# Down-projection in 19 uneven runs of pairs, its first operands and weights split before the up-projection's last sums

## The chip, the cores and the metric

The kernel runs on one core of a Trainium2 chip. The metric is the device time of one execution in microseconds (us); lower is better. One program holds a whole decoder layer; the change concerns its last stage and the seam in front of it.

## The reference

The layer has three parallel branches, a gated merge and an output projection, and ends with a normalised squared-ReLU MLP. Only this end matters here (1,024 tokens, model width 1,024, hidden width 4,096):

```python
x = x + merged @ w_out[l]
h2 = rms_norm(x, norm_mlp_g[l])
x = x + jnp.square(jax.nn.relu(h2 @ w_up[l])) @ w_down[l]
```

## The kernel before

All matrix products keep fp32 accuracy by splitting each operand into a high part (a cast on ScalarE) and a low part (a subtraction on VectorE) and issuing three matmuls per product (`mm3`, L130). `split` (L110) leaves both halves to the scheduler; `split2` (L105) pins the subtraction on VectorE (`self.V`, L69) behind whatever was traced before it on that engine. Matmuls are pinned the same way (L94). Every other instruction (ScalarE's, GpSimd's, the DMA issues of SyncE's queue, SP, and VectorE's where `nc.vector` is called) is placed on its engine by a scheduler at compile time; once placed, each engine runs its list in order.

Both MLP products use Strassen-Winograd: a 2x2 block product in seven products instead of eight. A **step** is one K-pair (256 rows of the contraction) for one group of outputs: 7 products x 3 = 21 matmuls of 128x128 by 128x512.

- **Up-projection** (`wino`, L1309): 16 groups u of 4 steps. After each group, `combine` (L1328) copies the first of seven PSUM banks to SBUF on ScalarE and folds the other six with seven VectorE adds into four 128x512 blocks (tiles u and c). `use_up` (L1537) multiplies them by the row norm (on GpSimd for the last group, u = 15), applies ReLU and square on ScalarE, stores three of them (tile rq), forms four Winograd sums (`wino_t`, tile xts, L1258) and stores those too. Group u's result, seven blocks in the scratch tensor r_d, is K-pair u of the down-projection.
- **Down-projection** (`down`, L1586): 4 output groups g x 16 pairs = 64 steps. A pair's operand is loaded (`xdma`), then split (`xsplit`, tiles xd) into one of four SBUF places, chosen by pair number mod 4; a weight tile is loaded (`raw`, tile wraw), gets four Winograd sums on GpSimd (`wino_s`, L1277) and is split (`wsp`, tiles wo); there are three places for each kind. The steps are cut into **passes**: one output group over consecutive pairs, collected in seven PSUM banks. Pass p takes group p mod 4 and pairs p to p + 3, so there are 16 passes of 4, and pairs 16, 17 and 18 are pairs 0, 1 and 2 loaded a second time. At the end of a pass, seven accumulators in SBUF take up the banks: in a group's first pass three by ScalarE copies and four by VectorE adds onto the residual, which four DMAs (acc<-x1_d, traced as acc<-x_d, L1698) put there and one subtraction prepares. Eight banks are cycled, so product j + 1 of a pass needs the bank that product j of the pass before has left. In each group's last pass the sums are folded and stored; group 3's accumulators are folded ahead, at the end of pass 11, so that the very last pass has a short end.
- **Places**: SBUF space of the down stage is laid over that of the up stage. The operand place of pair 0 is in three parts, dx00, dx01 and dx02; dx02 lies on the last two up-projection weight buffers. Pairs 1, 2 and 3 lie on up operands 0, 1 and 2, which are last read in the last four up steps. Accumulators of groups 0 and 1 lie on up operand 3, those of groups 2 and 3 mostly on the tiles u, c, xts and rq.

What sets the order at the seam is therefore the scheduler: the last group's `combine`, its post-processing, the stores of r_d and the first loads and splits of the down stage are all placed by it, except that `split2` subtractions and accumulations are pinned behind what was traced before them.

Of the kernel before, what the change touches and what calls it, by code (L numbers as in the profile page):

```python
# [10 lines left out]
F32 = mybir.dt.float32  # L11
F32R = mybir.dt.float32r
AF = mybir.ActivationFunctionType
# [4 lines left out]
P = 128  # L18
# [13 lines left out]
def f32(ap):  # L32
    return ap.bitcast(F32)
# [40 lines left out]
class Layer:  # L74
# [9 lines left out]

    pinned = False
    nmm, kmm = 0, 2
    marks = {}

    def pin(self, ins):
# [6 lines left out]
    def transpose(self, out, x):  # L96
        self.pin(self.nc.tensor.transpose(out, x, self.ident))  # L97

    def other_tile(self):
        return self.pmm.tile([P, 512], F32, tag=f"mm{1 - self.nmm}", name=self.name("pr"))  # L100

# [2 lines left out]

    def split2(self, hi, lo, src):  # L105

        self.A.copy(hi, src)  # L107
        self.V.tensor_sub(lo, src, f32(hi))

    def split(self, hi, lo, src, scale=None):  # L110

        nc = self.nc
        if scale is None:
            a = nc.scalar.copy(hi, src)  # L114
            return a, nc.vector.tensor_sub(lo, src, f32(hi))  # L115
# [1142 lines left out]
    def wino_t(self, b, V):  # L1258

        G = self.nc.gpsimd  # L1260
        t = self.xtp.tile([P, 4, 512], F32, tag="xt", name=self.name("xts"))
        V.tensor_sub(t[:, 0], b[:, 0], b[:, 1])
        G.tensor_sub(t[:, 2], b[:, 2], b[:, 0])
        V.tensor_sub(t[:, 1], b[:, 2], t[:, 0])
        V.tensor_sub(t[:, 3], b[:, 3], t[:, 1])
        return t

    def wino_x(self, kp, load):
# [40 lines left out]
    def wino(self, ws, load, use, first, parts):  # L1309


        V, A = self.V, self.A
# [3 lines left out]
        raw, wsp, W = self.wino_steps([ws[u][:, kp] for u, kps in runs for kp in kps], self.wrp, self.wop, 3)  # L1316
# [11 lines left out]
        def combine(ms, psum):  # L1328

            m1, m2, m6, m7, m4, m5, m3 = ms  # L1330
            u2, c11, u3, c21 = m1, m2, m7, m4
            if psum:
                u2, c11, u3, c21 = (tl(n) for n in ("u2", "c11", "u3", "c21"))
                A.copy(u2, m1)
            V.tensor_add(c11, u2, m2)
# [5 lines left out]
            V.tensor_add(u2, u2, m3)  # L1341
            return u2, c11, u3, c21


# [1 line left out]
        n = -1  # L1346
        for r, (u, kps) in enumerate(runs):
            bank = lambda j: f"p{(7 * r + j + 4) % 8}"
            ps = [self.pw.tile([P, 512], F32, tag=bank(j), name=self.name(f"p{j}")) for j in range(7)]
# [18 lines left out]
            elif r == 2:  # L1368
# [66 lines left out]
    def tail(self):  # L1435
        tc, nc, a = self.tc, self.nc, self.a
        V, G = nc.vector, nc.gpsimd
        half = lambda d, f, hf: d[f, :, hf * 512 : (hf + 1) * 512]
# [8 lines left out]
        with ExitStack() as c0:  # L1447
# [9 lines left out]
            with ExitStack() as c1:  # L1457
                E = lambda *x, **k: c1.enter_context(tc.tile_pool(*x, **k))
                self.pmm, self.kmm, self.nmm = Banks(E, "pmm2"), 8, 3
                if True:  # L1460
# [11 lines left out]
                    hi = [[mtp.tile([P, 512], F32R, name=f"mh{k}_{hf}") for hf in range(2)] for k in range(NK)]  # L1472
                    mg, lo = {}, {}
# [43 lines left out]
            with ExitStack() as c1:  # L1517
                E = lambda *x, **k: c1.enter_context(tc.tile_pool(*x, **k))
                one_ = lambda n: E(name=n, bufs=1)
# [17 lines left out]
                def use_up(u, cs):  # L1537

                    b = self.xrp.tile([P, 4, 512], F32, tag="xr", name=self.name("rq"))
                    V_, M = (nc.vector, G) if u == 15 else (self.V, self.V)  # L1540
                    for i in (1, 3, 2, 0):
                        hf = i % 2
                        M.tensor_mul(cs[i], cs[i], rb[:, hf * 512 : (hf + 1) * 512])
                        self.A.activation(cs[i], cs[i], AF.Relu)
                        self.A.activation(b[:, i], cs[i], AF.Square)
# [3 lines left out]
                    nc.sync.dma_start(self.rd[u, :, 3:7], t)  # L1549
                    yield  # L1550

                def rstd():
# [33 lines left out]
    def down(self):  # L1586

        tc, nc, a = self.tc, self.nc, self.a
        V = nc.vector
        half = lambda d, f, hf: d[f, :, hf * 512 : (hf + 1) * 512]  # L1590
        with ExitStack() as c1:
            one_ = lambda n: c1.enter_context(tc.tile_pool(name=n, bufs=1))
# [27 lines left out]
            kp = lambda q: q if q < 16 else q - 16  # L1620
# [6 lines left out]
            raw, wsp, W = self.wino_steps([a["wdown"][g][:, kp(q)] for g, q in steps], wr, wo, 2)  # L1627
# [5 lines left out]
            def xdma(q):  # L1633

                X[q] = []
                for pool, i, n in xp[q % 4]:
                    t = pool.tile([P, n, 2, 512], F32R, tag=f"x{i}", name=self.name("xd"))
                    nc.sync.dma_start(f32(t[:, :, 1]), self.rd[kp(q), :, i : i + n])
                    X[q].append(t)

            def xsplit(q, parts=(0, 1, 2), split=self.split2):
                for i, t in enumerate(X[q]):
                    if i in parts:
                        split(t[:, :, 0], t[:, :, 1], f32(t[:, :, 1]))

            def operand(q, j):
                for t in X[q]:
                    if j < t.shape[1]:
                        return t[:, j, 0], t[:, j, 1]
                    j -= t.shape[1]  # L1650

            def side(n):
# [24 lines left out]
            n = -1  # L1677
            seen = set()
            for p, (g, qs) in enumerate(passes):
                A = acc[g]  # L1680
                new = g not in seen
                seen.add(g)
                ps = [
                    self.pw.tile([P, 512], F32, tag=f"p{(7 * (self.nwino + p) + j + 4) % 8}", name=self.name(f"p{j}"))
                    for j in range(7)
                ]
# [6 lines left out]
                    if q != qs[-1]:  # L1693
                        side(n)
                if new:

                    for j, f, hf in ((1, 0, 1), (6, 0, 0), (4, 1, 1), (5, 1, 0)):
                        nc.sync.dma_start(A[j], half(self.x1d, 2 * g + f, hf))  # L1698
                    V.tensor_sub(A[6], A[6], A[5])

                if p <= last - 4:
                    for j in range(7):
                        if new and j in (0, 2, 3):
                            A_.copy(A[j], ps[j])
                        else:
                            V.tensor_add(A[j], A[j], ps[j])
                    side(n)
                    if p == last - 4:
                        add = V.tensor_add
                        a1, a2, a6, a7, a4, a5, a3 = A  # L1710
                        add(a2, a2, a1)
                        add(a6, a6, a1)
                        add(a7, a7, a6)
                        add(a4, a4, a7)
                        add(a7, a7, a5)
                        add(a6, a6, a5)
                        add(a6, a6, a3)
                    continue
                o = lambda f, hf, t: nc.sync.dma_start(half(self.out, 2 * g + f, hf), t)
                add = V.tensor_add  # L1720
                a1, a2, a6, a7, a4, a5, a3 = A
# [15 lines left out]
                else:  # L1737

                    m1, m2, m6, m7, m4, m5, m3 = ps
# [203 lines left out]
```

## Time and profile before

| | us |
|---|---|
| median of 3 runs (2176.92 to 2179.55) | 2178.19 |
| the profiled execution, its own time | 2178.26 |
| its span, first to last instruction | 2176.5 |
| up-projection's matmuls, first start to down's first | 1541.1 to 1852.3 |
| down-projection's matmuls, first start to last end | 1852.3 to 2171.9 |

A row of a timeline is: start, length, engine, source line, operation, written tile <- read tiles, shape, count; brackets hold the idle time before the row and the instruction that ended it. Rows of `L94 ... p<-xd,wo` are down-projection matmuls; `xd` rows are operand splits, `wo` rows weight splits, `acc` rows accumulations. VectorE is DVE, ScalarE ACT, GpSimd POOL, TensorE PE; SPq is SyncE's DMA queue. A view of windows gives each engine's busy time in a stretch and PEclk, the TensorE clock granted, as a share of full speed.

### The profile page before, as it was taken

Reading aid. Unit: us, or ns where it says so; the run is one execution under the profiler, and the core shown is the slowest. Engines: PE = TensorE matmul, PEld = TensorE weight load, DVE = VectorE, ACT = ScalarE, POOL = GpSimd, SP = SyncE. Lnnn points to the kernel's source line nnn. Section 1 sums busy time; section 2 is a strip of 40 time slices with the busy share of each in tenths; the row PEclk is TensorE's granted clock in tenths of the full one; section 3 lists DMA queues with packets and bytes.
Section 4 is the critical chain, followed back from the end, with each engine's and each line's share of the span. In section 5 each row is a group of like instructions: output and inputs, shape, how many; then the busy total and the mean of one; then the engine's idle time right before and its main releaser. Section 6 shows DMA issues by size and latency. Waiting matters only on the chain.

```text
span 2176.5 us, 30687 instructions
## 1 busy us (share of the span) xinstructions
PE 2140.9 (98%) x11049; PEld 1850.3 (85%) x11049; DVE 1415.2 (65%) x2674; ACT 998.6 (46%) x1998; POOL 567.2 (26%) x736
## 2 busy tenths in 40 slices
PE   7999999999999999999999999999999999899999
PEld 5888888898899999999878888888888788688887
DVE  6644475574557787777655342645688987767789
ACT  6543354453346666666544220314444444543332
POOL 2100000000111111111031002103655674655552
PEclk9999999999999999999999999999999999999999
DMA  6115122131433333323344543426434544844444
GB/s 240 44 65 169 36 92 69 40 102 37 170 92 93 93 98 98 95 77 85 107 159 150 199 165 106 146 94 218 134 141 169 184 160 174 304 155 160 152 137 166
DMA packets 137357, 281.45 MB, mean 129 GB/s; under 512 B 13137, under 2 KB 29814, under 8 KB 135158
## 3 DMA queue, kind: packets, MB, share of 16 engines
q1 hardware_dynamic: 130870, 259.58, 37.4%
q10 hardware_dynamic: 6336, 19.93, 2.3%
q8 instruction: 87, 1.43, 0.3%
q14 instruction: 64, 0.52, 0.1%
HBM read 182.95 MB, written 71.34 MB: 117 GB/s over the span
## 4 chain that ended last, share of the span: by engine, by line
PE 88%; DVE 4%; DMA 2%; ACT 2%; issue 1%; POOL 1%; SPq 0%; DVEq 0%; ACTq 0%; POOLq 0%
PE mm L94 52%; PE p L94 23%; PE sc L94 6%; PE po L94 3%; PE tp L97 3%; DVE acc L69 1%; PE pr L97 1%; DVE u L69 1%; DVE wo L69 1%; DMA hx<-hc_d 0%; DVE c L69 0%; PE tp L94 0%; DVE w L115 0%; DMA ngb<-g_dng 0%; DMA xd<-r_d 0%
## 5 line engine op out<-in xcount | busy, mean ns | idle before, releaser
L94 PE MATMUL mm<-w,hT 128*128 128x384 f32 (+3 forms) x2496 | 468.7, 330 | 0.7 <-DVE dsg L118 0.7
L94 PE MATMUL mm<-hT,w 128*128 128x512 f32 x1680 | 408.1, 393 | 1.2 <-ACT gt L492 1.2
L94 PEld LDWEIGHTS mm<-w,hT 128*128 128x128 f32 x2496 | 388.6, 189 | 10.9 <-DVE dsg L118 0.9
L94 PEld LDWEIGHTS mm<-hT,w 128*128 128x128 f32 x1680 | 308.3, 188 | 61.4 <-ACT gt L492 1.7
L94 PE MATMUL p<-xd,wo 128*128 128x512 f32 x1344 | 311.4, 393 | 8.2 <-DVE acc L69 1.9
L94 PEld LDWEIGHTS p<-xd,wo 128*128 128x128 f32 x1344 | 254.1, 190 | 65.3 <-DVE xd L69 2.6
L94 PE MATMUL p<-xo,wo 128*128 128x512 f32 x1344 | 307.0, 390 | 1.5 <-DVE u L69 1.5
L94 PEld LDWEIGHTS p<-xo,wo 128*128 128x128 f32 x1344 | 251.6, 188 | 55.6 <-DVE u L69 3.1
L94 PE MATMUL mm<-kt,w 128*128 128x512 f32 x1152 | 261.5, 389 | 0.0
L94 PEld LDWEIGHTS mm<-kt,w 128*128 128x128 f32 x1152 | 216.1, 188 | 45.2 <-DVE kt L115 0.3
L107 ACT CAST wo<-wraw 128x896 fp32r<-128x896 f32 x124 | 116.9, 945 | 217.6 <-PE p L94 105.2
L114 ACT CAST w<-raw 128x256 fp32r<-128x256 f32 (+3 forms) x272 | 139.8, 546 | 140.4 <-PE mm L94 112.0
L115 DVE TENSOR_TENSOR w<-raw,w 128x256 fp32r<-128x256 f32 (+3 forms) x272 | 158.7, 607 | 51.7 <-ACT w L114 51.0
L69 DVE TENSOR_TENSOR wo<-wraw,wo 128x896 fp32r<-128x896 f32 x124 | 144.8, 1182 | 56.6 <-ACT wo L107 56.6
L1280 POOL TENSOR_TENSOR wraw<-wraw 128x128 f32<-128x128 f32 x128 | 94.4, 738 | 240.0 <-DMA wraw<-in_wdown 101.2
L1029 ACT ACTIVATE dpe<-sc,dst,drr 128x256 f32<-128x256 f32 (+7 forms) x128 | 106.7, 834 | 96.7 <-DVE dst L1025 93.6
L140 POOL TENSOR_SCALAR hss<-hss 128x4 f32<-128x4 f32 x8 | 4.1, 515 | 409.0 <-ACT mscr L774 409.0
L1021 DVE CUSTOM_DVE_ANT_0 sc<-sc,tmask 128x256 f32<-128x256 f32 (+7 forms) x128 | 97.1, 759 | 13.8 <-PE sc L94 13.1
L1283 POOL TENSOR_TENSOR wraw<-wraw 128x128 f32<-128x128 f32 x128 | 90.0, 703 | 10.0
L94 PE MATMUL sc<-dk,dq 128*128 128x512 f32 (+3 forms) x384 | 91.9, 347 | 0.0
L107 ACT CAST xd<-xd 128x1536 fp32r<-128x1536 f32 (+2 forms) x38 | 58.3, 1535 | 65.8 <-DMA xd<-r_d 65.8
L1282 POOL TENSOR_TENSOR wraw<-wraw 128x128 f32<-128x128 f32 x128 | 87.1, 681 | 0.0
(313 smaller groups left out, 3078.8 us busy)
## 6 DMA issues: line engine op xcount, KB each, us to landing
dk<-dsg SPq DMA_DIRECT2D x64, 256.0 KB, 4.2
wraw<-in_wup SPq DMA_DIRECT2D x64, 256.0 KB, 3.0
r_d<-xts SPq DMA_DIRECT2D x16, 1024.0 KB, 4.1
wraw<-in_wdown SPq DMA_DIRECT2D x64, 256.0 KB, 3.0
xd<-r_d SPq DMA_DIRECT2D x19, 768.0 KB, 7.1
xd<-r_d SPq DMA_DIRECT2D x14, 1024.0 KB, 6.2
raw<-in_wd SPq DMA_DIRECT2D x32, 384.0 KB, 3.3
kraw<-y SPq DMA_DIRECT2D x24, 512.0 KB, 5.3
```

The lines of the kernel that those rows point to most:

```text
L69: return self.tc.keep_in_program_order(f(*a, **k))
L94: self.pin(self.nc.tensor.matmul(out, l, r, start=start, stop=stop))
L97: self.pin(self.nc.tensor.transpose(out, x, self.ident))
L107: self.A.copy(hi, src)
L114: a = nc.scalar.copy(hi, src)
L115: return a, nc.vector.tensor_sub(lo, src, f32(hi))
L140: g.tensor_scalar(r, ss, 1.0 / width, EPS, op0=ALU.mult, op1=ALU.add)
L1021: V.tensor_tensor_reduce(out=sc[:, 0:n], in0=sc[:, 0:n], in1=self.tmask[:, D - n : D], scale=1.0, scalar=-3.0e38, op0=ALU.add, op1=ALU.max ...
L1029: nc.scalar.activation(pe[c][:, 0:n], sc[:, 0:n], AF.Exp, bias=t8[:, 2 + c : 3 + c], scale=rr[:, i, c : c + 1], accum_out=t8[:, 4 + c : 5 ...
L1280: G.tensor_add(r[:, 4], r[:, 0], r[:, 3])
L1282: G.tensor_sub(r[:, 6], r[:, 1], r[:, 0])
L1283: G.tensor_sub(r[:, 7], r[:, 2], r[:, 5])
```

## The change

- The passes become 19, of 2, 2, 3, 4, then 3, 4, 4, 4, then 4, 4, 4, 4, then 3, 3, 2, and last 4, 3, 3, 4 pairs. Every pair is loaded once; the second loads of pairs 0, 1 and 2 go.
- Explicit steps for the operand splits (`SPLIT`) and for group 3's early folding (`FOLD`) take the place of fixed distances.
- dx02 moves to free space at the end; a dummy tile (dfree) fills its old place. Pair 0's three parts are split behind the Winograd sums of up groups 10, 11 and 12.
- Order edges (`behind`: at compile time, an engine's list gets the first argument after the second): pair 1's load before the store of up group 14; pair 1's casts before `combine`'s first copy, and weight 1's subtraction before its first add, for the last up group; weight 2's subtraction after its last add; the last group's four ReLUs after the first pass's ScalarE copies and its Winograd sums after that pass's VectorE adds; the residual loads of groups 0 and 1 before the store of up group 15, and pair 3's load after that store. The residual of group g + 1 is loaded one pass ahead.

```diff
+    def behind(self, ins, first):
+        self.tc.add_manual_dep(
+            ins, first.name,
+            mybir.DependencyInfo(mybir.DependencyClass.NoSync, mybir.DependencyReason.DATA), reason="order",
+        )
...
-            x02, wr = one_("dx02"), Ring(wr)
+            one_("dfree").tile([P, 2048], F32, name="dfree")
+            wr = Ring(wr)
             wo = Ring([one_(f"dwo{i}") for i in range(3)])
-            x00 = one_("dx00")
+            x00, x02 = one_("dx00"), one_("dx02")
...
-            passes = [(p % 4, tuple(range(p, 4 + p))) for p in range(16)]
+            to = lambda g, lo, hi: (g, tuple(range(lo, hi + 1)))
+            passes = [to(0, 0, 1), to(1, 0, 1), to(2, 0, 2), to(3, 0, 3)]
+            passes += [to(0, 2, 4), to(1, 2, 5), to(2, 3, 6), to(3, 4, 7)]
+            passes += [to(0, 5, 8), to(1, 6, 9), to(2, 7, 10), to(3, 8, 11)]
+            passes += [to(0, 9, 11), to(1, 10, 12), to(2, 11, 12)]
+            passes += [to(0, 12, 15), to(1, 13, 15), to(2, 13, 15), to(3, 12, 15)]
...
-                    if q >= 3 and n == use1[q] - 3:
-                        xsplit(q, (0,))
-                    if q >= 3 and n == use1[q] - 2:
-                        xsplit(q, (1, 2))
+                    for i, at in enumerate(SPLIT.get(q, ())):
+                        if n == at:
+                            xsplit(q, (0,) if i == 0 else (1, 2))
+                for t, s in FOLD.get(n, ()):
+                    V.tensor_add(acc[3][t], acc[3][t], acc[3][s])
...
+            SPLIT = {2: (3, 4), 3: (7, 8), 4: (10, 11), 5: (13, 14)}
+            SPLIT.update({q: (4 * q - 7, 4 * q - 6) for q in range(6, 13)})
+            SPLIT.update({13: (45, 46), 14: (48, 49), 15: (50, 51)})
             xdma(0)
             raw()
             raw()
-            xsplit(0, split=self.split)
+            turned = self.turned[-16:]
+            for i, u in enumerate((10, 11, 12)):
+                xsplit(0, (i,), self.split, turned[u][1])
             wsp(0, self.split, False)
-            xdma(1)
+            self.behind(self.stored[14], xdma(1))
             xsplit(1, split=self.split)
+            self.behind(self.first_copy, self.cast)
             wsp(0)
+            self.behind(self.first_add, self.sub)
+            wsp(0)
+            self.behind(self.sub, self.last_add)
             xdma(2)
-            xsplit(2, (0,))
-            wsp(0)
-            xsplit(2, (1, 2))
-            xdma(3)
...
                 if new:
-                    for j, f, hf in ((1, 0, 1), (6, 0, 0), (4, 1, 1), (5, 1, 0)):
-                        nc.sync.dma_start(A[j], half(self.x1d, 2 * g + f, hf))
+                    if g == 0:
+                        residual(0)
+                        loaded = residual(1)
+                        self.behind(self.stored[15], loaded)
+                        with tc.issue_after(self.stored[15]):
+                            xdma(3)
+                    elif g < 3:
+                        residual(g + 1)
                     V.tensor_sub(A[6], A[6], A[5])
...
+                    if p == 0:
+                        for i in range(4):
+                            self.behind(self.relus[15, i], c.ins)
+                        self.behind(self.turned[-1][0], v.ins)
                     side(n)
```

More of the change, by code (lines that the diff above doesn't have):

```diff
@@ L86 @@
     nmm, kmm = 0, 2
+    turned, stored, relus = [], {}, {}
     marks = {}
@@ L105, in split2 @@
     def split2(self, hi, lo, src):
-        self.A.copy(hi, src)
-        self.V.tensor_sub(lo, src, f32(hi))
+        self.cast = self.A.copy(hi, src).ins
+        self.sub = self.V.tensor_sub(lo, src, f32(hi)).ins
     def split(self, hi, lo, src, scale=None):
@@ L114, in split @@
             a = nc.scalar.copy(hi, src)
+            self.cast = a.ins
             return a, nc.vector.tensor_sub(lo, src, f32(hi))
@@ L1261, in wino_t @@
         t = self.xtp.tile([P, 4, 512], F32, tag="xt", name=self.name("xts"))
-        V.tensor_sub(t[:, 0], b[:, 0], b[:, 1])
+        first = V.tensor_sub(t[:, 0], b[:, 0], b[:, 1]).ins
         G.tensor_sub(t[:, 2], b[:, 2], b[:, 0])
         V.tensor_sub(t[:, 1], b[:, 2], t[:, 0])
-        V.tensor_sub(t[:, 3], b[:, 3], t[:, 1])
+        self.turned.append((first, V.tensor_sub(t[:, 3], b[:, 3], t[:, 1]).ins))
         return t
@@ L1333, in combine @@
                 u2, c11, u3, c21 = (tl(n) for n in ("u2", "c11", "u3", "c21"))
-                A.copy(u2, m1)
-            V.tensor_add(c11, u2, m2)
+                self.first_copy = A.copy(u2, m1).ins
+            self.first_add = V.tensor_add(c11, u2, m2).ins
             V.tensor_add(u2, u2, m6)
@@ L1340, in combine @@
             V.tensor_add(u2, u2, m5)
-            V.tensor_add(u2, u2, m3)
+            self.last_add = V.tensor_add(u2, u2, m3).ins
             return u2, c11, u3, c21
@@ L1618, in down @@
             acc = [accs[7 * g : 7 * g + 7] for g in range(4)]
-            kp = lambda q: q if q < 16 else q - 16
             self.pinned = True
             V, A_ = self.V, self.A
-            passes = [(p % 4, tuple(range(p, 4 + p))) for p in range(16)]
+            to = lambda g, lo, hi: (g, tuple(range(lo, hi + 1)))
[4 more added lines that the diff above has]
+            passes += [to(0, 12, 15), to(1, 13, 15), to(2, 13, 15), to(3, 12, 15)]
             last = len(passes) - 1
             steps = [(g, q) for g, qs in passes for q in qs]
-            raw, wsp, W = self.wino_steps([a["wdown"][g][:, kp(q)] for g, q in steps], wr, wo, 2)
+            raw, wsp, W = self.wino_steps([a["wdown"][g][:, q] for g, q in steps], wr, wo, 2)
             X, use1, use9 = {}, {}, {}
@@ L1637, in xdma, with xsplit @@
                     t = pool.tile([P, n, 2, 512], F32R, tag=f"x{i}", name=self.name("xd"))
-                    nc.sync.dma_start(f32(t[:, :, 1]), self.rd[kp(q), :, i : i + n])
+                    ins = nc.sync.dma_start(f32(t[:, :, 1]), self.rd[q, :, i : i + n]).ins
                     X[q].append(t)
-            def xsplit(q, parts=(0, 1, 2), split=self.split2):
+                return ins
+            def xsplit(q, parts=(0, 1, 2), split=self.split2, after=None):
                 for i, t in enumerate(X[q]):
                     if i in parts:
-                        split(t[:, :, 0], t[:, :, 1], f32(t[:, :, 1]))
+                        with tc.issue_after(after) if after else ExitStack():
+                            split(t[:, :, 0], t[:, :, 1], f32(t[:, :, 1]))
             def operand(q, j):
@@ L1650, in operand @@
                     j -= t.shape[1]
+            FOLD = {42: ((1, 0), (2, 0)), 46: ((3, 2), (4, 3)), 52: ((3, 5), (2, 5), (2, 6))}
             def side(n):
@@ L1666, in down, with residual @@
             raw()
-            xsplit(0, split=self.split)
+            turned = self.turned[-16:]
+            for i, u in enumerate((10, 11, 12)):
+                xsplit(0, (i,), self.split, turned[u][1])
             wsp(0, self.split, False)
-            xdma(1)
+            self.behind(self.stored[14], xdma(1))
             xsplit(1, split=self.split)
+            self.behind(self.first_copy, self.cast)
             wsp(0)
+            self.behind(self.first_add, self.sub)
+            wsp(0)
+            self.behind(self.sub, self.last_add)
             xdma(2)
-            xsplit(2, (0,))
-            wsp(0)
-            xsplit(2, (1, 2))
-            xdma(3)
+            def residual(g):
+                for j, f, hf in ((1, 0, 1), (6, 0, 0), (4, 1, 1), (5, 1, 0)):
+                    ins = nc.sync.dma_start(acc[g][j], half(self.x1d, 2 * g + f, hf)).ins
+                return ins
             n = -1
@@ L1703, in down @@
                         if new and j in (0, 2, 3):
-                            A_.copy(A[j], ps[j])
+                            c = A_.copy(A[j], ps[j])
                         else:
-                            V.tensor_add(A[j], A[j], ps[j])
-                    side(n)
[L1708 to L1717, printed above, removed]
+                            v = V.tensor_add(A[j], A[j], ps[j])
+                    if p == 0:
+                        for i in range(4):
+                            self.behind(self.relus[15, i], c.ins)
+                        self.behind(self.turned[-1][0], v.ins)
+                    side(n)
                     continue
```

4 lines of the change are left out of this document (2 added, 2 removed).

## The prediction, made before the changed kernel ran

> **What bounds the kernel now.** I read the page first: its share of busy time by engine says that TensorE is the engine to look at.
>
> ```profile
> span 2176.5 us, 30687 instructions
> PE 2140.9 (98%) x11049; PEld 1850.3 (85%) x11049; DVE 1415.2 (65%) x2674; ACT 998.6 (46%) x1998; POOL 567.2 (26%) x736
> ```
>
> With 98% busy nothing but a gap in the matmuls can be won, unless matmuls are removed, and the change removes none: 64 steps of 21 before and after. The second view is TensorE's timeline over the down stage.
>
> ```profile
> 1852.31 1.52 PE L94 MATMUL p<-xd,wo 128*128 128x512 f32 x6
> 1854.39 0.97 PE L94 MATMUL p<-xd,wo 128*128 128x512 f32 x3 [0.56 <-DVE c L69]
> 1856.11 2.51 PE L94 MATMUL p<-xd,wo 128*128 128x512 f32 x9 [0.76 <-POOL wraw L1281]
> 1859.04 10.52 PE L94 MATMUL p<-xd,wo 128*128 128x512 f32 x45 [0.42 <-DVE u L69]
> 1871.16 0.50 PE L94 MATMUL p<-xd,wo 128*128 128x512 f32 x1 [1.60 <-ACT wo L107]
> 1873.29 0.79 PE L94 MATMUL p<-xd,wo 128*128 128x512 f32 x1 [1.64 <-DVE xd L69]
> 1875.42 8.16 PE L94 MATMUL p<-xd,wo 128*128 128x512 f32 x25 [1.33 <-DVE wo L69]
> 1885.46 286.42 PE L94 MATMUL p<-xd,wo 128*128 128x512 f32 x1254 [1.88 <-DVE acc L69]
> ```
>
> The last row is one unbroken run of 1254 matmuls, 286.42 / 1254 = 0.2284 us each, so a step of 21 costs 4.80 us and nothing is to be won behind 1885.46 except at the very end. The 90 matmuls ahead of it should take 90 x 0.2284 = 20.56 us and take 1885.46 - 1852.31 = 33.15. **12.6 us are lost in the first four steps and the first change of pass.** By row: the first 18 matmuls take 6.73 us instead of 4.11 (2.6 lost); the next 45 take 12.12 with the gap behind them instead of 10.28 (1.8); the last 27 take 14.30 instead of 6.17 (8.1). The idle times in brackets sum only to 8.2; the rest is slow running, and the window view says why.
>
> ```profile
> 1874.00:1878.00 4.00, 2.67 (x7) 1.62 (x6) 4.00 (x4) 2.29 (x3) 1.60 (x2) 0.50 0.82 261
> ```
>
> The 0.50 is the granted clock: after three gaps in a row TensorE gets half its speed for some us. A gap costs more than its length.
>
> Third, who is late. VectorE's list at the seam:
>
> ```profile
> 1851.44 2.29 DVE L115 TENSOR_TENSOR xd<-xd 128x2048 fp32r<-128x2048 f32 x1 [0.16 <-ACT xd L114]
> 1853.65 0.68 DVE L69 TENSOR_TENSOR c<-u,p 128x512 f32<-128x512 f32 x1
> 1854.25 1.16 DVE L69 TENSOR_TENSOR wo<-wraw,wo 128x896 fp32r<-128x896 f32 x1
> 1855.33 1.47 DVE L69 TENSOR_TENSOR u<-u,p 128x512 f32<-128x512 f32 x2
> 1868.94 0.69 DVE L1262 TENSOR_TENSOR xts<-rq 128x512 f32<-128x512 f32 x1 [2.93 <-ACT rq L1545]
> 1871.23 2.01 DVE L69 TENSOR_TENSOR xd<-xd 128x1536 fp32r<-128x1536 f32 x1
> 1874.03 1.34 DVE L69 TENSOR_TENSOR wo<-wraw,wo 128x896 fp32r<-128x896 f32 x1
> 1875.29 2.54 DVE L69 TENSOR_TENSOR xd<-xd 128x2048 fp32r<-128x2048 f32 x1
> 1884.11 0.69 DVE L69 TENSOR_TENSOR acc<-acc,acc 128x512 f32<-128x512 f32 x1 [5.29 <-DMA acc<-x_d]
> ```
>
> Three stories stand here. First, the up-projection's last `combine` starts only at 1853.65, behind pair 1's split, and weight 1's split cuts in after its first add, so the banks come free late. Second, weight 3 and pair 3 are split at 1871 to 1877.8, behind the last group's post-processing, though step 3 should start at 1852.31 + 3 x 4.80 = 1866.7. Third, the end of pass 0 waits for the residual. GpSimd and SP say why the second and third are so late:
>
> ```profile
> 1832.28 0.46 POOL L1283 TENSOR_TENSOR wraw<-wraw 128x128 f32<-128x128 f32 x1
> 1863.93 2.39 POOL L1283 TENSOR_TENSOR wraw<-wraw 128x128 f32<-128x128 f32 x1
> 1866.29 1.29 POOL L1543 TENSOR_TENSOR u<-u,rb 128x512 f32<-128x512 f32 x1
> ```
>
> ```profile
> 1838.22 2.57 SPq L1638 DMA_DIRECT2D xd<-r_d  x3
> 1860.03 1.46 SPq L1638 DMA_DIRECT2D xd<-r_d  x3
> 1874.18 0.33 SPq L1549 DMA_DIRECT2D r_d<-xts  x1
> 1874.91 1.65 SPq L1294 DMA_DIRECT2D wraw<-in_wdown  x2
> 1876.61 2.05 SPq L1698 DMA_DIRECT2D acc<-x_d  x4
> ```
>
> The last multiplication of group 15 sits on GpSimd until 1866.29 behind weight sums; ScalarE's last ReLU waits for it, and the splits of weight 3 and pair 3 stand behind that ReLU in ScalarE's list. The store of group 15 blocks SP from the end of the row at 1860.03, 1861.5, to 1874.18; two weight loads and the residual's loads stand behind it.
>
> **The change part by part.**
>
> *Combine and splits at the seam.* Pair 1's casts and weight 1's subtraction now stand ahead of `combine`, then seven adds run unbroken, then weight 2's subtraction. Pair 0's third part no longer has its load among the three issued at 1838.22 nor its cast among the three here, which all end before the late split of 1851.44:
>
> ```profile
> 1847.06 4.36 ACT xd L114 x3
> ```
>
> Of the three casts the smallest goes (1024 of 4608 columns, 1.0 us), so pair 1's subtractions end near 1852.7 instead of 1853.73; weight 1's 1.16 us follow; the first add starts at 1853.9 at the worst, and some 2 us sooner if a load a fifth smaller also lands sooner. The down stage's third product (from 1852.31 + 6 x 0.2284 = 1853.7) needs that add done. Each further add takes about 0.7 us, a product 0.685, so they keep pace. Loss left: 0 to 1.0 of 2.6; I take 0.4, nearer the low end, since the load shrinks.
>
> *Short first passes.* Pairs 2 and 3 are first needed in steps 6 and 10 (at 1881 and 1900) instead of 2 and 3. Pair 3's split of 1871 to 1877.8 would be in time even unmoved. What is late next is weight 3, needed at 1866.7: its place is free after step 0 (1857.1), its cast no longer stands behind a ReLU, its subtraction stands behind the first pass's adds. The pass ends at 1861.9, the last add 0.7 later, the subtraction 1.2 later, 1863.8: 2.9 us in hand.
>
> *Residual.* Its loads need up operand 3, free at 1852.31, and are now put before the store of group 15. These are the times from issue to landing in the seam, beside 12 weight loads:
>
> ```profile
> acc<-x_d SPq DMA_DIRECT2D x16, 256.0 KB, 5.6
> wraw<-in_wdown SPq DMA_DIRECT2D x12, 256.0 KB, 5.6
> ```
>
> Four issues of 0.5 us and 5.6 to land give 1860; the first add onto them can start when product 1 of step 1 is done, 1858.5, and must not start later than 1862.5 (its bank is needed a whole step less one product on). So this stall goes, unless a weight load that waits for weight 2's subtraction is put ahead: then 1858.5 + 2 + 5.6 = 1866, 3.5 us late. I take 0.6.
>
> *New waits.* Group 15's ReLUs now follow the first pass's third ScalarE copy, its Winograd sums that pass's last add (1862.6). Both come before the multiplication that ends at 1866.29 + 1.29 = 1867.6 in the trace, so if that keeps its time, the sums start at 1868.94 and the store is issued at 1874.18 as now; if it comes sooner, some 3 us sooner. So 1871 to 1875. Queued behind it on SP: pair 3's load (needed at 1900, covered), the residual of group 2, and perhaps weight loads from 7 on. Group 2's residual needs the store landed, then its own landing; at 5.6 each that is 1882 to 1886, wanted at 1882.5 and not later than 1886.5. Weight 7, if put behind the store: 1875 + 5.6, four sums of 0.46 to 2.39 each, 2.3 for cast and subtraction: 1885 to 1892, wanted at 1885.9. Loss 0 to 6; I take 1.0, since a weight load is released by the split three weights ahead, and those of 3 and 4 come by 1866.
>
> *More passes, fewer loads.* The groups of the down stage give the prices:
>
> ```profile
> L69 DVE TENSOR_TENSOR xd<-xd 128x1536 fp32r<-128x1536 f32 (+2 forms) x38 | 74.0, 1954 | 0.7 <-ACT xd L107 0.6
> L69 DVE TENSOR_TENSOR wo<-wraw,wo 128x896 fp32r<-128x896 f32 x63 | 70.9, 1140 | 55.3 <-ACT wo L107 55.3
> L69 DVE TENSOR_TENSOR acc<-acc,p 128x512 f32<-128x512 f32 x100 | 67.1, 686 | 13.2 <-PE p L94 12.5
> ```
>
> Three more passes add 21 adds of 0.686 = 14.4 us to VectorE; the 38 parts are 17 whole pairs, 74.0 / 17 = 4.35 each, so three pairs fewer save 13.1. Net 1.3 us on an engine that has slack, but not evenly. The densest stretch is steps 42 to 49: 21 adds (14.4), 8 weights (9.1), pairs 13 and 14 (8.7), four folding adds (2.8), 35.0 of 38.4 us. Before, a pass of the last third already ran like this, with no gap in TensorE:
>
> ```profile
> 2110.00:2129.20 19.20, 19.20 (x86) 15.91 (x85) 19.00 (x22) 6.50 (x6) 9.46 (x16) 1.00 0.61 203
> 1755.00:1774.00 19.00, 15.21 (x19) 1.00 0.47 169
> ```
>
> The first row's third figure is VectorE at 19.00 of 19.20 us. 91% of a stretch is thus covered by a stretch that stood 99%; if a pass change were caught 1 to 4 us late, that would be the cost. I take 0.3.
>
> *Pair 0's split in the up stage.* It moves from the fourth and fifth group to groups 10 to 12. The second row above, of VectorE alone, is in those groups: 15.2 of 19.0 us, so the 2.3 us of the largest part fit. Where two of its parts are now, TensorE lost something:
>
> ```profile
> 1701.75 1.76 PE L94 MATMUL p<-xo,wo 128*128 128x512 f32 x6 [0.77 <-DVE u L69]
> 1703.93 148.53 PE L94 MATMUL p<-xo,wo 128*128 128x512 f32 x654 [0.42 <-DVE u L69]
> ```
>
> Gain 0 to 1.2 if they go, a loss as large if a part again meets a `combine`. I take 0.6 gained, as the parts now stand behind the sums, not amid the adds.
>
> *The end.* VectorE now runs late into the last pass:
>
> ```profile
> 2163.05 2.28 DVE L69 TENSOR_TENSOR xd<-xd 128x2048 fp32r<-128x2048 f32 x1
> 2171.27 2.08 DVE L69 TENSOR_TENSOR acc<-acc,p 128x512 f32<-128x512 f32 x3
> ```
>
> The last matmul ends at 1885.46 + 286.42 = 2171.88, and three adds still follow to 2173.35. The split at 2163 goes (its pair is not loaded again). The adds of the last product but one can then be done as it ends; one of them and its pause fall away: 0.7 us, at least 0.
>
> *Sum.* Of 12.6 lost, 0.4 + 0.6 + 1.0 = 2.0 stay: 10.6 gained. Up stage 0.6, end 0.7, densest stretch -0.3: 11.6. The profiled execution took 2178.26 (span 2176.5 and 1.76 around it), 0.07 from the median 2178.19, so the sum holds for the median: **2166.6**. Best case by the bounds: 12.6 + 1.2 + 0.7 = 14.5, 2163.7. All the worst ends at once (10.5 stay, up 1.2 and dense 4 lost, end 0) would be 3 over now; they have separate causes, so this case's upper end is one of them, the largest, 5 over my value: 2171.6.
>
> **Rivals.**
>
> *A, a stall of pass 1 or 2 stays.* The residual is late by 3.5 us, or the weights behind the store by 6, and the clock drops again for some us (2.4 were lost so in the row of 25 matmuls: 8.16 - 5.71). 2166.6 + 3 to 8 = 2170 to 2175. For it: the same resources are late now. Against: at the middle of its times each has some 2 us in hand.
>
> *B, GpSimd becomes the bound.* A sum of a weight took 0.46 us in one row and 2.39 in another, when VectorE was splitting an operand. At 2.39 each a weight costs 9.6 us against a step of 4.80, and the four multiplications add 5.2. If two weights in a row are held so, GpSimd falls 2 x 4.8 + 5.2 = 14.8 us behind; the splits run two steps ahead, which covers 9.6; 5.2 us are lost: 2171.8. Against: seven adds that read PSUM now run unbroken while GpSimd multiplies. [...]
>
> *C, slower: SP's list.* If weight load 5 too is placed behind the store of group 15, weight 5 (wanted at 1876.3) comes at 1875 + 5.6 + 1.8 to 9.6 + 2.3 = 1885 to 1892.5, 9 to 16 us late with the next weights on its heels, plus 2.4 of slow clock: 2165.6 (the sum without its 1.0) + 11 to 18 = 2177 to 2184, middle 2180. For it: this store blocks SP for 12.7 us in the trace, with two weight loads behind it. Against: weight 2's subtraction, which releases load 5, now stands right behind `combine`, some 12 us ahead of the store. It decides if that load is issued after 1866 at the latest (1876.3 - 2.3 - 1.8 - 5.6).
>
> *D, no change.* The gaps close and the densest stretch opens as many: 19 passes with VectorE full. It needs 12 us there, where my bound is 4.
>
> **How the numbers follow.** Less than 0.2%, 4.4 us, cannot be told from no change; so faster means under 2173.8, slower over 2182.6. Forecast 0.64, all faster. A 0.15, of which 0.12 faster. B 0.07, faster. C 0.08, half of it slower beyond the bound, half within. D 0.06, half within the bound, half beyond it, as 12 us there could as well be 18. Faster 0.64 + 0.12 + 0.07 = 0.83, lowered to 0.80 as the placed order isn't in the trace of before; slower 0.07; same the rest, 0.13. The range runs from the best bound, 2163.5, to 2174.0, by which B and nearly all of A end; C and D, and little else, are left out.
>
> **What would show it.** TensorE's timeline from 1852 on: the first 90 matmuls in 20.6 to 23 us and clock 1.00 throughout; the first add of `combine` by 1853.6 with six adds unbroken; weight 3 split near 1864; residual landed before 1862.5; the store of group 15 at 1871 to 1875 with weight load 5 ahead of it on SP. Steps 42 to 56 without a gap over 0.5. I am wrong if a gap with a clock of 0.50 is found in the first eleven steps, or if VectorE's list makes banks late at a pass of two or three steps.

## The result and the profile after

The changed kernel takes 2162.49 us (median of 6 runs, 2161.13 to 2164.96) against 2177.72 of the kernel before (6 runs): a ratio of 0.9931, 95% interval 0.9918 to 0.9944. Measured once more on another occasion it took 2161.88 against 2178.03, ratio 0.9924, 0.9909 to 0.9938. So it is faster, by 15 to 16 us; forecast were 11.6, and 2162.49 lies 1.0 us under the range.

The page of the changed kernel, the same two lines as before:

```profile
span 2159.3 us, 30669 instructions
PE 2133.7 (99%) x11049; PEld 1849.6 (86%) x11049; DVE 1421.0 (66%) x2688; ACT 987.2 (46%) x1991; POOL 578.5 (27%) x736
```

The matmul count is the same, VectorE does 14 instructions more, ScalarE 7 fewer. TensorE's timeline over the later part of the up stage and all of the down stage is two rows:

```profile
1682.12 167.91 PE L95 MATMUL p<-xo,wo 128*128 128x512 f32 x738 [0.35 <-DVE u L69]
1849.88 305.05 PE L95 MATMUL p<-xd,wo 128*128 128x512 f32 x1344
```

All 1344 matmuls of the down stage run in one piece: 0.2270 us each. The eight rows of before have become one, with no gap at all. Why is seen in VectorE's list and SP's list (here and below as in the prediction; a row with x2 merges two instructions):

```profile
1843.69 3.95 DVE L123 TENSOR_TENSOR xd<-xd 128x1536 fp32r<-128x1536 f32 x2
1847.56 1.08 DVE L69 TENSOR_TENSOR wo<-wraw,wo 128x896 fp32r<-128x896 f32 x1
1848.57 0.68 DVE L69 TENSOR_TENSOR c<-u,p 128x512 f32<-128x512 f32 x1
1857.98 1.48 DVE L69 TENSOR_TENSOR acc<-acc,acc 128x512 f32<-128x512 f32 x1 [2.74 <-DMA acc<-x_d]
1861.78 1.28 DVE L69 TENSOR_TENSOR wo<-wraw,wo 128x896 fp32r<-128x896 f32 x1
1863.20 0.73 DVE L1270 TENSOR_TENSOR xts<-rq 128x512 f32<-128x512 f32 x1
```

```profile
1848.68 0.35 SPq L1302 DMA_DIRECT2D wraw<-in_wdown  x1
1850.07 5.65 SPq L1702 DMA_DIRECT2D acc<-x_d  x8
1856.08 0.33 SPq L1302 DMA_DIRECT2D wraw<-in_wdown  x1
1863.09 0.33 SPq L1302 DMA_DIRECT2D wraw<-in_wdown  x1
1866.56 0.32 SPq L1557 DMA_DIRECT2D r_d<-xts  x1
```

Pair 1 and weight 1 are split by 1848.6; `combine`'s first add starts at 1848.57, 1.31 us **before** the first down-projection matmul, where it started 1.34 us behind it. The residual has landed by 1858, weight 3 is split at 1861.78, and the store of group 15, issued 7.6 us earlier in the span than before (5.2 us earlier against the first down matmul), finds the residual loads and weight loads 4, 5 and 6 ahead of it.

Where the 17.2 us between the two profiled spans come from: 0.5 ahead of the up stage, where nothing was changed; 1.9 between the gap near 1682 and the first down-projection matmul (169.66 to 167.76); 14.5 in the down stage (319.57 to 305.05, first start to last end); 0.25 behind the last matmul. The stages before the up-projection vary by up to 6 us between executions (the up stage began between 1539.7 and 1546.2 in the traces below), so the experiments are read by these stage lengths first. One trace stands behind each length; the down stages of the two traces of the changed kernel differ by 0.7 us, so less than about 1 us between two runs is not told apart.

### The profile page after: what moved, and what is told of

It reads as the page before. It is cut to its first block, busy times and chain, and to the rows that moved or that the text cites. A ratio compares the mean times of both kernels' runs of the same rounds, so it can differ in the third digit from the quotient of the medians.

```text
span 2159.3 us, 30669 instructions
## 1 busy us (share of the span) xinstructions
PE 2133.7 (99%) x11049; PEld 1849.6 (86%) x11049; DVE 1421.0 (66%) x2688; ACT 987.2 (46%) x1991; POOL 578.5 (27%) x736
## 4 chain that ended last, share of the span: by engine, by line
PE 92%; DVE 2%; DMA 2%; ACT 1%; issue 0%; POOL 0%; SPq 0%; DVEq 0%; ACTq 0%; POOLq 0%
PE mm L95 52%; PE p L95 27%; PE sc L95 6%; PE po L95 3%; PE tp L98 3%; PE pr L98 1%; DMA hx<-hc_d 0%; PE tp L95 0%; DVE acc L69 0%; DVE w L123 0%; DMA ngb<-g_dng 0%; PE sc L98 0%; DMA wib<-g_dwi 0%; DVE u L69 0%; DMA raw<-in_wd 0%
## 5 line engine op out<-in xcount | busy, mean ns | idle before, releaser
L95 PE MATMUL p<-xd,wo 128*128 128x512 f32 x1344 | 305.0, 390 | 0.0
L69 DVE TENSOR_TENSOR wo<-wraw,wo 128x896 fp32r<-128x896 f32 x124 | 151.6, 1232 | 46.5 <-ACT wo L114 46.5
L1288 POOL TENSOR_TENSOR wraw<-wraw 128x128 f32<-128x128 f32 x128 | 94.2, 736 | 214.5 <-DMA wraw<-in_wdown 74.6
L1290 POOL TENSOR_TENSOR wraw<-wraw 128x128 f32<-128x128 f32 x128 | 96.7, 756 | 0.0
L1289 POOL TENSOR_TENSOR wraw<-wraw 128x128 f32<-128x128 f32 x128 | 90.5, 707 | 0.0
L69 DVE TENSOR_TENSOR acc<-acc,p 128x512 f32<-128x512 f32 x121 | 80.3, 685 | 15.0 <-PE p L95 14.4
```

What stands on the lines that cost most here:

```text
L69: return self.tc.keep_in_program_order(f(*a, **k))
L95: self.pin(self.nc.tensor.matmul(out, l, r, start=start, stop=stop))
L1288: G.tensor_add(r[:, 4], r[:, 0], r[:, 3])
L1289: G.tensor_sub(r[:, 5], r[:, 4], r[:, 1])
L1290: G.tensor_sub(r[:, 6], r[:, 1], r[:, 0])
```

## The experiments

Theory 1: several lists are late at the seam, each edge and the short passes remove a part, and each gap left costs slow clock besides. Theory 2: the gain comes from fewer loads and splits. Theory 3: the order edges bring it and the passes do not matter. "Up" is the length from the gap near 1682 to the first down-projection matmul, "down" from there to the end of the last; the ratio is to the kernel before.

| run | up | down | median us | ratio (95% interval) |
|---|---|---|---|---|
| before | 169.66 | 319.57 | 2177.72 | 1 |
| changed | 167.76 | 305.05 | 2162.49 | 0.9931 (0.9918 to 0.9944) |
| e0_changed_again | 167.71 | 305.74 | 2161.88 | 0.9924 (0.9909 to 0.9938) |
| e1_old_passes | 167.66 | 312.77 | 2170.54 | 0.9966 (0.9953 to 0.9979) |
| e2_passes_only | 169.66 | 322.74 | 2180.84 | 1.0012 (1.0003 to 1.0022) |
| e3_dx02_back | 167.72 | 314.03 | 2169.92 | 0.9962 (0.9948 to 0.9977) |
| e4_group15_free | 167.69 | 308.85 | 2166.25 | 0.9945 (0.9931 to 0.9960) |
| e5_residual_late | 167.77 | 308.72 | 2166.35 | 0.9944 (0.9929 to 0.9958) |
| e6_pair0_free | 171.63 | 305.45 | 2165.44 | 0.9937 (0.9920 to 0.9954) |
| e7a_hold_combine | 167.67 | 306.23 | 2164.20 | 0.9932 (0.9917 to 0.9947) |
| e7b_hold_combine | 167.65 | 311.94 | 2169.34 | 0.9956 (0.9941 to 0.9971) |
| e8_halved | 167.79 | 305.20 | 2161.97 | 0.9926 (0.9912 to 0.9940) |
| e9_idle_load | 167.68 | 312.12 | 2168.44 | 0.9956 (0.9940 to 0.9972) |
| e10_dx02_last | 167.47 | 311.19 | 2167.55 | 0.9952 (0.9938 to 0.9967) |
| e11_load_no_wait | 167.65 | 306.44 | 2164.15 | 0.9937 (0.9922 to 0.9951) |
| e12_wait_no_load | 167.66 | 307.35 | 2162.76 | 0.9929 (0.9912 to 0.9945) |

**The changed kernel again.** No edit.

> The changed kernel once more, beside the next three on the same chip. All theories: 2161 to 2165, down stage (first down-projection matmul to the end of the last) 305.0 us without a gap, up stage 309.2 to 309.4 as in every trace with the edges on pair 0.

As expected but for one gap of 0.22 us in step 7, counted from 0, where the fourth pass begins and waits for a ScalarE copy; the down stage was 305.74.

**Old passes, all edges.**

```diff
-            passes = [to(0, 0, 1), to(1, 0, 1), ...
+            passes = [(p % 4, tuple(range(p, 4 + p))) for p in range(16)]
```

The second loads, the splits of pair 2 ahead of the passes and the folding at the end of pass 11, which belong to these passes, are back too.

> All order edges and the moved dx02 kept, but the 16 passes of four pairs and the second loads of pairs 0 to 2 put back. Theory 1 (stalls at the seam, with the slow clock that they leave; edges and short passes each remove a part): pair 2 is wanted in step 2 (about 1859.5) and pair 3 in step 3 (1864.3) again, and their splits need 8 us of VectorE behind a combine that ends at 1854, so 2 to 6 us are lost there and the time is 2164 to 2169. Theory 2 (fewer loads and splits bring the gain, edges are worth little): 2173 to 2178. Theory 3 (the edges alone bring it): 2161 to 2164.

Down is 7.7 us longer than changed, 6.8 shorter than before. ScalarE's list shows what is late:

```profile
1868.36 0.94 ACT L114 CAST wo<-wraw 128x896 fp32r<-128x896 f32 x1 [6.54 <-POOL wraw L1291]
1869.21 3.27 ACT L114 CAST xd<-xd 128x1536 fp32r<-128x1536 f32 x2
```

Weight 3 and, behind it, pair 3 are cast at 1868 and 1869, though step 3 was due at 1855.38 + 3 x 4.77 = 1869.7, with the VectorE halves still to come. Weight 3 waits for its sums on GpSimd, of which two took 1.97 and 2.51 us while VectorE split pair 2 (0.46 each in other rows), with group 15's last multiplication in between until 1867.9 (1.99 and 2.39 us beside the same split in the kernel before): the case of rival B, which the short passes avoid, as they split pair 2 only at 1871. Theory 3 falls; the loss is a little over theory 1's 2 to 6.

**New passes, no edges.**

```diff
-            self.behind(...)            (all of them, and both issue_after)
-            one_("dfree").tile([P, 2048], F32, name="dfree")
+            x02 = one_("dx02")
-                        residual(0); loaded = residual(1) ...
+                    for j, f, hf in ((1, 0, 1), (6, 0, 0), (4, 1, 1), (5, 1, 0)):
+                        nc.sync.dma_start(A[j], half(self.x1d, 2 * g + f, hf))
```

> The 19 passes with their split steps and foldings, but no order edge, dx02 in its old place and residual and pair 3 loaded where the kernel before loads them. Theory 1: combine again starts behind a late split (2.6 us lost), weight 3 again stands behind the last ReLU and the residual behind the store of group 15 (together 4 to 9 lost), so 2168 to 2175, with a clock below 1.00 at the seam. Theory 2: 2161 to 2165. Theory 3: 2176 to 2179.

No gain at all: down 322.74, 3.2 us longer than before. It holds 16 pair loads instead of 19, so theory 2 falls. But this is also worse than theory 1 had it, and than theory 3. TensorE, VectorE and SP:

```profile
1864.93 11.20 PE L95 MATMUL p<-xd,wo 128*128 128x512 f32 x36 [1.37 <-DVE u L69]
1883.45 296.09 PE L95 MATMUL p<-xd,wo 128*128 128x512 f32 x1296 [7.33 <-DVE acc L69]
```

```profile
1882.11 0.69 DVE L69 TENSOR_TENSOR acc<-acc,acc 128x512 f32<-128x512 f32 x1 [5.86 <-DMA acc<-x_d]
```

```profile
1861.71 1.42 SPq L1719 DMA_DIRECT2D acc<-x_d  x3
1876.33 0.32 SPq L1557 DMA_DIRECT2D r_d<-xts  x1
1876.69 0.43 SPq L1719 DMA_DIRECT2D acc<-x_d  x1
```

Three of the four residual loads were issued at 1861.7, the fourth stood behind the store of group 15 until 1876.69. The short first pass wants the residual two steps sooner, so the wait for pair 3 has only turned into one of 7.3 us for the residual.

**dx02 back.**

```diff
-            one_("dfree").tile([P, 2048], F32, name="dfree")
-            wr = Ring(wr)
+            x02, wr = one_("dx02"), Ring(wr)
```

> The changed kernel with dx02 back on the last two up-projection weight buffers, so that the third part of pair 0 is loaded at about 1836 and split beside pair 1. Theory 1: 0.5 MB more to load and 1.2 us more of VectorE ahead of combine, which had 2.0 us in hand (first add done at 1849.25, its bank wanted at 1851.25): no change or up to 2 us, 2162 to 2165. Theory 2: no change. Theory 3 (this place is one of the edges that bring it): 2165 to 2168.

9.0 us, all theories missed. TensorE, and ScalarE's casts:

```profile
1854.33 15.39 PE L95 MATMUL p<-xd,wo 128*128 128x512 f32 x59 [2.74 <-DVE c L69]
1871.87 291.83 PE L95 MATMUL p<-xd,wo 128*128 128x512 f32 x1279 [2.15 <-DVE wo L69]
```

```profile
1845.73 4.36 ACT L121 CAST xd<-xd 128x1024 fp32r<-128x1024 f32 x3 [4.38 <-DMA xd<-r_d]
```

ScalarE stands until 1845.73 for the load of the third part; in the changed kernel pair 1's casts began at 1841.45. `combine` comes 5.2 us later against the first matmul, and the weight load that weight 1's split releases comes as late, which is the second gap. Four more runs ask what made the load late.

**The place in the lists.** dx02 as in e3, the third part's split behind pair 1's.

```diff
             xsplit(1, split=self.split)
+            with tc.issue_after(self.cast):
+                xsplit(0, (2,), self.split, self.xsub)
```

> dx02 back in its old place as before, but the split of pair 0's third part is put behind pair 1's split on both engines. If the place in the lists was the cost, pair 1 is split while the third part lands, combine starts 1 us later than in the changed kernel instead of 5, and the down stage is 305 to 307. If bandwidth was, it stays at 311 to 314.

Down 311.19: the lists were not it, pair 1's own second part landed 5 us late against the first down matmul. (The third part's split still stands ahead of `combine` here, so what its place in the lists costs by itself is not shown.)

**An idle load.** The changed kernel with a load that nothing reads:

```diff
+            nc.sync.dma_start(dfree[:, 0:1024].rearrange("p (k n) -> p k n", k=2), self.rd[0, :, 5:7])
             self.behind(self.stored[14], xdma(1))
```

> The changed kernel with a 0.5 MB load that nothing reads, put beside the load of pair 1 into the space where dx02 was. dx02 in its old place made the down stage 9.0 us longer. If that came from the bandwidth of half a megabyte more, this kernel loses most of it: down stage 309 to 314. If it came from the third part standing first in ScalarE's and VectorE's lists while its load lands last, the down stage stays within 305 to 306.5.

Down 312.12, 7.1 longer. SP's list shows that more than bytes were added:

```profile
1835.45 0.38 SPq L1650 DMA_DIRECT2D xd<-r_d  x1
1838.46 0.33 SPq L1691 DMA_DIRECT2D dfree<-r_d  x1
1838.84 0.43 SPq L1650 DMA_DIRECT2D xd<-r_d  x1
```

The idle load waits until the last up weight in that place is split and holds back pair 1's second part, which is issued 3.0 us later against the first down matmul.

**Bytes without the wait, the wait without the bytes.**

```diff
+            spare = one_("dspare").tile([P, 1024], F32, name="dspare")     (e11: 0.5 MB, waits for nothing)
...
+            with tc.issue_after(ins):                                      (ins is pair 1's load)
+                extra = nc.sync.dma_start(spare.rearrange("p (k n) -> p k n", k=2), self.rd[0, :, 5:7]).ins
...
+            nc.sync.dma_start(dfree[:, 0:128], self.rd[0, :, 5, 0:128])    (e12: 64 KB, in the old place)
```

> The changed kernel with the same idle 0.5 MB load, but into space that nothing used before it, put on SP right behind both parts of pair 1, so that it waits for nothing and holds nothing up; it shares the DMA engines with pair 1's second part. If the bytes cost the 7.1 us of the idle load before, the down stage is 309 to 312 here; if SP's wait did, 305 to 306.

> The same place on SP as the idle load before (between the two parts of pair 1, into the old space of dx02, which is free only after the last up weight's split near 1838.4), but of 64 KB instead of 0.5 MB. If the wait on SP made pair 1's second part late, its issue moves from 1836.3 to 1838.8 again and the down stage is 308 to 312; if the bytes did, 305 to 306.5.

The cast of pair 1's second part, in the changed kernel, with the idle load, in e11 and in e12:

```profile
1843.28 1.92 ACT L121 CAST xd<-xd 128x2048 fp32r<-128x2048 f32 x1 [0.36 <-DMA xd<-r_d]
```

```profile
1847.28 1.91 ACT L121 CAST xd<-xd 128x2048 fp32r<-128x2048 f32 x1 [4.70 <-DMA xd<-r_d]
```

```profile
1844.78 1.91 ACT L121 CAST xd<-xd 128x2048 fp32r<-128x2048 f32 x1 [1.17 <-DMA xd<-r_d]
```

```profile
1845.28 1.91 ACT L121 CAST xd<-xd 128x2048 fp32r<-128x2048 f32 x1 [2.96 <-DMA xd<-r_d]
```

This cast comes 6.6, 2.3, 5.8 and 4.0 us ahead of the first down matmul. So the bytes behind pair 1 cost the cast 0.8 us, the wait 2.6, the wait with the bytes ahead of pair 1's second part 4.3; the down stage lost 1.4, 2.3 and 7.1. Neither of the first two alone makes the loss. In e11 `combine` still starts 0.6 us ahead of the first down matmul, and TensorE meets only three gaps of 0.17 to 0.33 us further on; in e12 `combine` makes gaps of 0.38 and 0.43. Both together make one of 2.37, and the next gap follows (2.14, for the weight that was loaded late). In e9 all of this is waiting: its granted clock stays at 1.00 in both places, while in e3 the clock falls as well, to 0.65 in the 3.7 us behind its first gap and to 0.58 in the 3.5 us behind its second.

The two parts are not cleanly taken apart. Pair 1's second part was issued 3.0 us late in e9, but only 1.9 in e12 and 1.7 in e3 and e10, where the up weight's split ended sooner; and e11's bytes stand behind that part, not ahead of it. Bytes ahead of it without a wait were not run, and e10 (5 us with a wait of 1.7) and e9 (4.3 with one of 3.0) give no one price for them.

**Group 15 free.**

```diff
-                    if p == 0:
-                        for i in range(4):
-                            self.behind(self.relus[15, i], c.ins)
-                        self.behind(self.turned[-1][0], v.ins)
```

> The changed kernel without the edges that hold the ReLUs and the Winograd sums of group 15 behind the first pass. Theory 1: the ReLUs go back ahead of a weight's cast and the first pass's copies on ScalarE and wait there for GpSimd's multiplications (till 1859 now); with short passes only weight 3 (wanted at 1864.3) is at risk: 2162 to 2167. Theory 2: no change, 2161 to 2165. Theory 3: 2168 to 2172.

3.8 us, as theory 1 had it, by another wait than it named: the ReLUs hold up the first pass's copies.

```profile
1862.59 20.26 PE L95 MATMUL p<-xd,wo 128*128 128x512 f32 x88 [1.72 <-ACT acc L1736]
```

**Residual late.**

```diff
-                    if g == 0: residual(0); loaded = residual(1) ...
+                    for j, f, hf in ((1, 0, 1), (6, 0, 0), (4, 1, 1), (5, 1, 0)):
+                        nc.sync.dma_start(A[j], half(self.x1d, 2 * g + f, hf))
```

and pair 3's load ahead of the passes.

> The changed kernel, but the residual of each group is loaded at its own pass, and pair 3 ahead of the passes, without the edges that tie them to the store of group 15. Theory 1: SP meets that store first and the residual lands 5 us or more behind the end of the first pass; product 3 of step 2 wants it by 1861: 3 to 8 us lost with the slow clock behind it, 2166 to 2171. Theory 2: no change, 2161 to 2165. Theory 3: 2166 to 2172, the same as theory 1.

3.7 us; the size was right, the reason not. The loads went out at 1852.1, ahead of the store, but behind pair 3's load, and landed at 1863.95, while the changed kernel's first subtraction of the residual started at 1857.98 (13.3 and 8.1 us behind the first down matmul):

```profile
1865.29 294.12 PE L95 MATMUL p<-xd,wo 128*128 128x512 f32 x1296 [3.56 <-DVE acc L69]
```

**Pair 0 free.**

```diff
-            for i, u in enumerate((10, 11, 12)):
-                xsplit(0, (i,), self.split, turned[u][1])
+            xsplit(0, split=self.split)
```

> The changed kernel without the edges that hold the three splits of pair 0 behind up groups 10 to 12. The up stage took 311.2 us before and 309.1 changed. Theory 1: two parts are split near 1690 to 1700 again and the 2.1 us of the up stage come back, the seam stays clean: 2163 to 2166. Theories 2 and 3: the up stage keeps 309, 2161 to 2164.

The up stage loses 3.9 us, nearly twice what was expected, the down stage nothing to speak of (0.4). The gaps are 0.76 and 0.76; some 1.7 are clock, which reads 0.97 and then 0.60 in the last two rows, of the windows view; and some 0.5 lie in the 78 matmuls ahead, which take 18.34 us as in the kernel before:

```profile
1700.87 0.97 PE L95 MATMUL p<-xo,wo 128*128 128x512 f32 x3 [0.76 <-DVE u L69]
1702.61 150.95 PE L95 MATMUL p<-xo,wo 128*128 128x512 f32 x657 [0.76 <-DVE c L69]
```

```profile
1699.00:1703.00 4.00, 2.48 (x9) 1.36 (x8) 3.90 (x6) 0.50 (x1) 1.86 (x3) 0.97 0.46 174
1703.00:1707.00 4.00, 4.00 (x12) 2.76 (x11) 3.90 (x6) 1.21 (x2) 3.00 (x6) 0.60 0.04 9
```

**Combine held.** One fill (e7a) or three (e7b):

```diff
+            for _ in range(1):
+                self.sub = V.memset(dfree, 0.0).ins
             self.behind(self.first_add, self.sub)
```

> The changed kernel with one fill of an unused 128x2048 tile on VectorE between weight 1's split and the first add of the last combine (some 1 to 2 us). By the trace of the changed kernel that add may come 2.0 us later before TensorE waits. Theory 1: no loss, or less than 0.7: 2162 to 2163. Theory 2 and 3 say nothing of it; if combine were timed to the limit, the loss is the fill's length.

> The same with three fills (3 to 6 us). Theory 1: TensorE stands for the length less 2.0 us, so 1 to 4 us; the clock after it tells what a gap costs beyond its length: if the wait alone counts, span 2160 to 2163; if half clock follows, up to 2 us more.

The first add came 2.2 and 6.8 us later against the first matmul; down lost 1.2 and 6.9. The first add by itself had the 2.0 in hand: 6.8 us late, it made a gap of 4.66. The lead of `combine` as a whole is about 1 (2.2 late, 1.2 lost): the later adds start 0.78 us apart and lose on the products of 0.68, where the prediction had them keep pace. Of the second, 4.66 is a gap and some 2 are clock (1338 matmuls in 305.75 us, where 0.2270 each make 303.7):

```profile
1857.49 305.75 PE L95 MATMUL p<-xd,wo 128*128 128x512 f32 x1338 [4.66 <-DVE c L69]
```

```profile
1857.50:1861.00 3.50, 3.50 (x8) 2.80 (x9) 3.15 (x5) 0.45 (x1) 3.38 (x5) 0.50 0.82 316
```

**Passes halved.**

```diff
-            passes += [to(0, 5, 8), to(1, 6, 9), to(2, 7, 10), to(3, 8, 11)]
+            passes += [to(0, 5, 6), to(0, 7, 8), to(1, 6, 7), to(1, 8, 9)]
+            passes += [to(2, 7, 8), to(2, 9, 10), to(3, 8, 9), to(3, 10, 11)]
```

> The changed kernel with the four passes over steps 26 to 41 cut in halves: the same matmuls in the same order, 28 adds of 0.686 us more on VectorE (19.2 us in 76 us). VectorE is busy some 80% of that stretch, so if it bounds the number of passes, it goes over 100% and TensorE loses up to 5 us: down stage 306 to 310. If short passes cost nothing but their adds' cover, 305.

Nothing: 305.20. VectorE alone, first of e8, then of the changed kernel:

```profile
1970.00:2046.00 76.00, 69.45 (x82) 1.00 0.46 152
```

```profile
1970.00:2046.00 76.00, 52.62 (x53) 1.00 0.45 152
```

VectorE had 52.6 of 76 us to do, not the 80% expected, and at 69.5 (91%) TensorE still meets no gap.

## Why the prediction was wrong, step by step

The direction and the places were right, the sum was 3.6 to 4.6 us short by the medians and 5.6 by the spans, because three terms were mis-sized.

1. **"Nothing is to be won behind 1885.46 except at the very end."** This step failed. The row of 1254 matmuls was taken as dense, and its mean, 0.2284, as the full rate. A timeline merges rows that have no gap between them, and slow running is no gap. The window over its first 4.5 us in the kernel before has 13 starts at a clock of 0.63:

```profile
1885.46:1890.00 4.54, 4.54 (x13) 3.61 (x14) 4.54 (x6) 0.00 (x0) 1.13 (x3) 0.63 0.77 278
```

   At the rate of the changed kernel 1254 matmuls take 284.65, so 1.8 us lay in that row, behind the gap before it, and the 90 ahead of it lost 12.7: 14.5 in all, not 12.6. The lower end of the range failed with it: it was the best case, 12.6 + 1.2 + 0.7, and with 14.5 here and the 1.9 of point 3 that case is 2161.1, below both medians.
2. **Seam, 2.0 us to stay: measured 0** (0.7 in the repeat). Times are compared against the first down matmul, as that itself came 2.4 us sooner. `combine`'s first add was put 1.6 us behind it at the worst and 0.4 ahead of it at the best; it came 1.31 ahead. That was mis-sized in the step on dx02, which counted one cast of 1.0 us and a smaller load, 1 to 3 us, where e3 shows 5.2. The old place makes a wait on SP in front of pair 1's second part and puts its bytes ahead of that part, 9.0 us with all that follows. The residual and weight 3, though, came no sooner than forecast. The first subtraction of the residual started 8.1 us behind the first matmul (forecast 7.7), and in e11, where it started 9.8 behind, TensorE waited. Weight 3's split ended 13.2 behind (forecast 11.5) and was wanted at 14.3. So these two stalls went with little to spare. Group 15's multiplications, put 15.3 us behind the first matmul by their old time, were done 9.0 behind it, and the store was issued 16.7 behind it where 18.7 to 22.7 were forecast. The four multiplications stand in one run, with no weight's sums between:

```profile
1852.99 3.41 POOL L1551 TENSOR_TENSOR c<-c,rb 128x512 f32<-128x512 f32 x2
1856.37 2.55 POOL L1551 TENSOR_TENSOR u<-u,rb 128x512 f32<-128x512 f32 x2
```

   So rivals A, B and C did not come up; C's point of decision held (load 5 was issued at 1856.08). Beside `combine`'s unbroken adds (1848.57 to 1853.80) eight weight sums of GpSimd took 0.46 or 0.47 us each.
3. **Pair 0's split, 0.6 gained and 1.2 at most: measured 1.9**, and 3.9 against the scheduler's own choice in e6. The bound was taken from two idle times in brackets. The row ahead of them belongs to the term: 78 matmuls in 18.33 us, which at 0.2270 take 17.7.

```profile
1682.65 18.33 PE L94 MATMUL p<-xo,wo 128*128 128x512 f32 x78 [0.34 <-DVE u L69]
```

4. **The densest stretch, -0.3: measured 0.** The prediction counted VectorE at 35.0 of 38.4 us in steps 42 to 49; in the changed kernel it is busy 36.6 of 38.2, and TensorE has no gap there:

```profile
2050.20:2088.40 38.20, 36.61 (x41) 1.00 0.56 188
```

5. **The end, 0.7 gained: measured 0.25.** The late split is gone, and VectorE stands idle ahead of the last pass's adds, yet the last three adds stand nearly as they stood:

```profile
2154.18 2.08 DVE L69 TENSOR_TENSOR acc<-acc,p 128x512 f32<-128x512 f32 x3
```

   They end 1.33 us behind the last matmul (2154.93), before 1.47. They follow one another on the last two products; the split did not make them late.

The three mis-sizings make 1.9 + 2.0 + 1.3 = 5.2, less 0.45 at the end and plus 0.3: 5.05, and 11.6 + 5.05 + 0.5 ahead of the up stage = 17.2, the difference of the spans. The medians differ by 15.2 and 16.2.

Beyond the terms: the prediction priced the parts as a sum. They are not one. Edges and dx02's place alone bring 6.8 us of the down stage, the passes alone lose 3.2, both together bring 14.5. Which of them carry the 6.8 was not tried one by one with the old passes.

## What to carry to other kernels

When a wait is taken away, ask for each queue what is asked for next and by when; here shorter passes alone only exchanged a wait for an operand for a longer one for the residual. Take the full rate from a stretch whose granted clock reads 1.00 throughout (0.2270 us a matmul here, against 0.2284 over a row that begins at 0.63), and size a stall by lost matmuls against that rate, not by idle times in brackets. A buffer laid over one that is released late can cost more than its own transfer: in e12 a load of 64 KB there held back the load queued behind it, whose cast came 2.6 us late.

## What the runs showed of the hardware that was not expected

The granted clock followed a gap irregularly in these runs. A gap of 3.56 us (e5) left it at 1.00, and the 1296 matmuls behind it took 294.12, their full rate; one of 4.66 (e7b) was followed by 3.5 us at 0.50; two of 0.76 within 3 us (e6) by 4 us at 0.60. Gaps of one size differ too: behind 2.15 us in e3 the clock was 0.58, behind 2.14 us at the same place in e9 it was 1.00. The windows behind these two gaps, e3 first:

```profile
1871.90:1875.40 3.50, 3.50 (x10) 2.72 (x11) 2.63 (x3) 1.94 (x3) 1.41 (x2) 0.58 0.95 267
1870.30:1874.00 3.70, 3.70 (x16) 3.06 (x17) 3.08 (x4) 2.15 (x4) 1.43 (x2) 1.00 0.95 271
```

In e6 the clock dropped behind a stretch in which TensorE was busy 2.48 of 4 us. What in the gaps decides was not tried.
